# Projections of the attention as one continuous stream, one PSUM pool, and TensorE in program order

## The chip, the cores and the metric

The kernel runs on one core of a Trainium2 chip. The metric is the device time of one execution in microseconds (us). PE is TensorE (PEld its weight loads), DVE is VectorE, ACT is ScalarE, POOL is GpSimd, and SP is the engine that issues most DMAs.

## The reference

Two layers on a sequence of 1024 rows of width 1024, in float32. Layer 0 mixes with forgetting attention, layer 1 with a spatial gating MLP. A gated convolutional MLP follows each. The change touches layer 0's attention only:

```python
proj = h @ w_in                                   # 1024 x (4*1024 + 16)
q, k, v, o, fl = jnp.split(proj, [D, 2*D, 3*D, 4*D], axis=-1)
q = rmsnorm(q.reshape(B, S, 16, 64), q_gain); k = rmsnorm(k..., k_gain)
F = jnp.cumsum(log_sigmoid(fl + b_f), axis=1)
for qb in range(8):                               # blocks of 128 queries, causal
    logits = q_block @ k[:end].T * scale + F[t] - F[s], masked
    outs.append(softmax(logits) @ v[:end])
x = x + gate * ((att * sigmoid(o)) @ w_out)
```

## The kernel before

Every float32 operand of a product is split into a high and a low part (`pair`: ACT casts the high part at L126, DVE subtracts for the low part at L119), and each product is three matmuls (`mm3`, recorded at L104). A framework turns the program into one static instruction list per engine. Each engine executes its list in that order, waiting where an operand or a buffer isn't ready. Unless instructions are chained to each other, the framework's planner chooses the order of a list.

The attention runs over 8 pairs of heads, called p. For each pair the work is:

- the projection of q, k and v (`proj`): two halves of 512 rows, each of 4 blocks of 128 rows. A block is 8 steps of three matmuls with 384 columns, into a PSUM tile `pj`. A step is one `yield` of a generator. So one pair has 64 steps, or 192 matmuls. ACT copies `pj` to the tile `qkv` (L566). After a half, ACT squares it (L572), DVE sums (L574), takes a reciprocal root by a dozen small operations (L141 to L150) and multiplies (L580). The weights (8 pairs of `x` tiles) come through the buffer `fraw`;
- `heads_qk(rw, half)`: 8 transposes on PE into `ms` tiles, then ACT (L647, L653) and DVE (L649) write the operands `qq`, `kh`, `kl`. `heads_v` casts v into `w`;
- `scores(p, fb, qt)` for the 8 blocks of queries: matmuls into PSUM tiles `s`, DVE adds the bias that POOL prepared and takes the extreme (L715), ACT takes the exponential (L726), ACT or DVE divides (L730, L732);
- `values(p, g, hd)`: for each pair of key blocks up to 4 transposes into `ms`, the split into `pt` by ACT (L750) and DVE (L119), and a deferred `product` of up to 4 matmuls into the PSUM tile `pv`.

The projection of pair p+1 is the filler between the steps of pair p. `tick(w)`, called inside `scores` and `values`, draws about w steps of the generator `self.fill`. At the end of a pair `heads_qk(rw, 0)` stands ahead of `drain()` and `heads_qk(rw, 1)` follows shortly after. The generators only set the program's order; in this kernel the planner may place PE's instructions otherwise. For the last pair the filler is `out_early`, three quarters of the output projection, after `x_transposed` has brought x into the transposed layout. The rest of the output projection follows the attention.

PSUM holds three pools in the attention: 3 tiles `s`, 2 tiles `pj`, 1 tile `pv` (and 2 `ms`). Ahead of all this stand the norm, the projection of pair 0, the `o` projections and eight jobs that compute the modulation vectors (`ada_part`, L257 to L285: weights by DMA, a chain on DVE, then small matmuls at L277). The chain on `ms` tiles puts the first transposes of pair 0 behind the last of these jobs.

Of the kernel before, what the change touches and what calls it, by code (L numbers as in the profile page):

```python
# [18 lines left out]
P = 128  # L19
# [7 lines left out]
SG = 8  # L27
# [40 lines left out]
class Trunk:  # L68


    def __init__(self, ctx, tc, **io):
        self.ctx, self.tc, self.nc = ctx, tc, tc.nc
        self.__dict__.update(io)
        self.chains = {}
        self.strict = self.ordered = False
        self.pending = None
        self.hooks = []
        self.ra, self.rx = "a", "X"
        self.n = 0
# [23 lines left out]
    def mm(self, out, lhsT, rhs, start, stop):  # L103
        i = self.nc.tensor.matmul(out, lhsT, rhs, start=start, stop=stop, skip_group_check=self.strict)  # L104
        return self.chain("pe", i) if self.strict else i
# [47 lines left out]
    def transpose4(self, srcs):  # L153

        ps = self.tile(self.ms, [P, 512], F32, "ms")
        for j, s in enumerate(srcs):
            i = self.nc.tensor.transpose(ps[: s.shape[1], j * P : (j + 1) * P], s, self.ident)  # L157
            if j == 0:
                self.chain("ms", i)
        return ps  # L160
# [182 lines left out]
    def fox(self):  # L343
# [9 lines left out]
        with ExitStack() as es:  # L353
# [20 lines left out]
            def ps1(pool, tag):  # L374
                return pool.tile([P, 512], F32, tag=tag, name=self.name(tag))
# [22 lines left out]
            def raw_pieces():  # L398
# [7 lines left out]
                return [T([P, 2, 2, 256], F32, "pt", 2) for _ in range(2)]  # L406
# [65 lines left out]
            for p in range(3):  # L472
                for half in range(2):
                    acc[p, half] = ps1(*((ps_s, "s") if p == 0 else (ps_p, "pj")) if p < 2 else (ps_s, "s") if half else (ps_v, "pv"))
# [28 lines left out]
            def o_out(p, half, ps):  # L503
                t = T([P, 512], F32, "pt", 2)
# [7 lines left out]
            def o_proj(p):  # L512
                w = o_weights(3 * D + p * P)
                ps = [ps1(ps_s, "s"), ps1(ps_p, "pj")]
# [15 lines left out]
            def weights(p):  # L530
                ws = []
                n = 400 if p == 0 else 384
                for k0 in range(0, KT, 2):
                    raw = T([P, 2, 400], F32, "fraw", 2)
                    for t in range(3):
                        i = nc.sync.dma_start(
                            raw[:, :, t * P : (t + 1) * P],
                            w_in[k0 * P : (k0 + 2) * P, t * D + p * P : t * D + (p + 1) * P].rearrange(
                                "(k p) f -> p k f", p=P
                            ),  # L540
# [3 lines left out]
                    if p == 0:  # L544
                        nc.sync.dma_start(
                            raw[:, :, 384:], w_in[k0 * P : (k0 + 2) * P, 4 * D :].rearrange("(k p) f -> p k f", p=P)
                        )
                    for j in range(2):
                        t = self.xslot([P, 2, 400], F32R)
                        ws.append(self.pair(t[:, :, :n], raw[:, j, :n], "x"))  # L550
                return ws

            def proj(p, ws, rw):

                n = 400 if p == 0 else 384
                for half in range(2):
                    r = T([P, 4, 384], F32, "qkv", 3)
                    for s in range(4):
                        ps = ps1(ps_p, "pj")
                        ss = slice(s * P, (s + 1) * P)  # L560
                        for k in range(KT):
                            self.mm3(
                                ps[:, :n], [(h[half, k][0][:, ss], h[half, k][1][:, ss], *ws[k])], k == 0, k == KT - 1
                            )
                            yield
# [54 lines left out]
            self.fill, self.due = iter(()), 0.0  # L620

            def tick(w):
                self.due += w
                while self.due >= 1:
                    self.due -= 1
                    next(self.fill, None)

            def drain():
                for _ in self.fill:
                    pass  # L630
                self.due = 0.0

# [29 lines left out]
            def heads_v(rw):  # L662
                v = self.wslot([P, NST, 256])
                for half in range(2):
                    vs = rw[half][:, :, 256:384].rearrange("p s (g d) -> p s g d", d=DH)
                    vd = v[:, 4 * half : 4 * half + 4, :].rearrange("p s (g d) -> p s g d", d=DH)
                    i = nc.scalar.copy(vd[:, :, 0:4:3, :], vs)
                    if half == 0:
                        self.chain("w", i)
                    self.split_lo(vd[:, :, 1:3, :], vs, vd[:, :, 0:4:3, :])  # L670
                return v
# [12 lines left out]
            def scores(p, fb, qt):  # L684
# [22 lines left out]
                for j, (c0, c1) in enumerate(zip(cuts, cuts[1:])):  # L707
                    n = c1 - c0
                    pss = [ps1(ps_s, "s") for _ in range(2)]
# [24 lines left out]
            def values(p, g, hd, v):  # L734
# [7 lines left out]
                pv = ps1(ps_v, "pv")  # L742
                for kt in range(0, 2 * g + 2, 2):
# [5 lines left out]
                    pt = T([P, 2, 512], F32R, "pt", 2)  # L749
# [37 lines left out]
            self.fill = proj(0, weights(0), rw)  # L787
# [33 lines left out]
            def out_early():  # L821
                for ps in (range(4), range(4, PC)):
                    for n in range(2):
# [4 lines left out]
                        for half in range(2):  # L828
                            for m in range(4 * n, 4 * n + 4):
                                yield from out_mm(ps1(ps_p, "pj"), ps, m, half)  # L830

            def x_transposed():
                self.xt = {(k, half): self.xslot([P, D]) for half in range(2) for k in range(4)}
                for half in range(2):
                    xs = []
                    for st in range(4 * half, 4 * half + 4):
                        t = self.hslot(F32).rearrange("p a f -> p (a f)")
                        self.chain("h", nc.sync.dma_start(t, self.x[0, st * P : (st + 1) * P, :]))
                        xs.append(t)
                    for k in range(KT):  # L840
                        ps = self.transpose4([t[:, k * P : (k + 1) * P] for t in xs])
                        o = self.xt[k % 4, half][:, k // 4 * 512 : (k // 4 + 1) * 512]
                        i = nc.scalar.copy(o, ps)
                        if k < 4:
                            self.chain("x", i)

            fb = f_rows(0)
            heads_qk(rw, 0)
            heads_qk(rw, 1)
            v = heads_v(rw)  # L850
            for p in range(8):
                if p < 7:
                    rw = []
# [7 lines left out]
                if p == 0:  # L861
                    scores(p, fb, 0)
                else:
                    values(p - 1, 3, 1, v0)
                    v = heads_v(rw0)
                scores(p, fb, 1)
                for g in range(3):
                    scores(p, fb, 2 * g + 2)
                    values(p, g, 0, v)
                    scores(p, fb, 2 * g + 3)  # L870
                    values(p, g, 1, v)
                v0, rw0 = v, rw
                if p < 7:
                    fb = f_rows(p + 1)
                    heads_qk(rw, 0)
                    drain()
                values(p, 3, 0, v)
                if p < 7:
                    heads_qk(rw, 1)
                    scores(p + 1, fb, 0)  # L880
                else:
                    values(p, 3, 1, v)
            flush()
            drain()
            for i in range(2):
# [3 lines left out]
            for half in range(2):  # L889
                for m in range(KT):  # L890
# [7 lines left out]
                    for _ in out_mm(banks() if banks else ps1(ps_p, "pj"), range(PC, 8), m, half):  # L898
# [648 lines left out]
    def sgu(self, jobs, every, scales, nxt):  # L1547
# [6 lines left out]
        bns = self.const.tile([P, NST, SG, 6], F32, name="bns")  # L1554
# [228 lines left out]
```

## Time and profile before

| | |
|---|---|
| median of 3 runs | 2730.57 us (2730.3 to 2733.01) |
| profiled execution | 2729.37 us, its span 2727.6 us |
| mean granted PE clock | 0.972 |
| PE, PEld, DVE, ACT, POOL busy | 2582.4, 2189.0, 2092.0, 1460.2, 164.5 us |
| last o projection on PE | ends at about 171.5 us |
| first transposes of pair 0's q and k | 193.6 us |
| the same of pairs 1 to 7 | 253.8, 328.0, 407.4, 479.8, 558.7, 630.2, 697.4 us |
| last matmul of the attention's output projection | ends at about 840 us |

The times of transposes are those of the first instruction of `heads_qk(rw, 0)` on PE. From one to the next is one period of the attention. The busy time of PE is an upper bound: matmuls overlap in the records, and at half clock the same matmul counts twice as long.

### The profile page before, as it was taken

How to read it: one execution, taken by the hardware profiler on the slowest of the kernel's cores; microseconds unless marked ns; L12 is line 12 of the kernel's file. 1: busy time of each engine (PE TensorE's matmuls, PEld its weight loads, DVE VectorE, ACT ScalarE, POOL GpSimd, SP SyncE). 2: the span in 40 equal slices, each digit the busy share in tenths (PEclk: the TensorE clock that was granted, in tenths of full speed). 3: DMA queues.
4: the chain of work that ended last, by engine and by line, in shares of the span. 5: the costliest groups of instructions: out<-in, count | busy, mean ns of one | idle time of the engine just before them, and what ended most of it. 6: DMA issues, size and time to landing. Idle time of an engine off the chain costs nothing.

```text
span 2727.6 us, 35317 instructions
## 1 busy us (share of the span) xinstructions
PE 2582.4 (95%) x12522; PEld 2189.0 (80%) x12522; DVE 2092.0 (77%) x3630; ACT 1460.2 (54%) x2310; POOL 164.5 (6%) x289
## 2 busy tenths in 40 slices
PE   6999899998797899999999999999999999999997
PEld 5999888886685788888888878888877788888886
DVE  7467777678786888898688777666788888877875
ACT  7327666667654554454545654554456455545444
POOL 1012222223100000000000000000000000000000
PEclk8999999988897999999999999999999999999999
DMA  6572111131113144554846346557552343337562
GB/s 229 169 241 62 43 51 47 45 110 62 56 55 124 62 132 135 161 159 151 289 152 206 97 136 184 188 183 278 158 173 85 112 143 101 124 101 283 162 198 91
DMA packets 315512, 377.61 MB, mean 138 GB/s; under 512 B 18760, under 2 KB 196040, under 8 KB 315336
## 3 DMA queue, kind: packets, MB, share of 16 engines
q1 hardware_dynamic: 315112, 375.30, 42.1%
q8 instruction: 98, 1.61, 0.2%
q14 instruction: 78, 0.64, 0.1%
q10 hardware_dynamic: 224, 0.06, 0.0%
HBM read 285.57 MB, written 89.72 MB: 138 GB/s over the span
## 4 chain that ended last, share of the span: by engine, by line
PE 82%; DVE 10%; ACT 2%; issue 2%; DMA 2%; SPq 1%; POOL 0%; DVEq 0%; POOLq 0%; ACTq 0%
PE bankX L104 19%; PE banka L104 17%; PE bankY L104 17%; PE pj L104 14%; PE ms L104 5%; PE s L104 3%; PE ms L157 3%; PE pv L104 2%; DVE ow L994 1%; DVE hc L994 1%; DVE x L994 1%; PE ms L1600 1%; DVE x L1479 1%; DVE rw L994 1%; SPq L421 1%
## 5 line engine op out<-in xcount | busy, mean ns | idle before, releaser
L981 ACT CAST ow<-rw 128x1024 fp32r<-128x1024 f32 (+1 forms) x438 | 398.7, 911 | 474.6 <-PE bankX L104 156.3
L994 DVE TENSOR_TENSOR ow<-rw,ow 128x1024 fp32r<-128x1024 f32 (+1 forms) x438 | 457.7, 1046 | 171.9 <-ACT ow L981 171.4
L104 PE MATMUL bankX<-hc,ow 128*128 128x512 f32 x1920 | 470.3, 393 | 17.5 <-DVE ow L994 9.6
L104 PEld LDWEIGHTS bankX<-hc,ow 128*128 128x128 f32 x1920 | 361.0, 189 | 95.4 <-DVE ow L994 11.4
L104 PE MATMUL banka<-hc,ow 128*128 128x512 f32 x1608 | 393.4, 393 | 6.5 <-ACT hc L981 2.8
L104 PE MATMUL bankY<-hc,ow 128*128 128x512 f32 x1584 | 388.6, 392 | 0.8 <-DVE ow L994 0.8
L104 PEld LDWEIGHTS banka<-hc,ow 128*128 128x128 f32 x1608 | 301.1, 189 | 71.3 <-ACT hc L981 4.4
L104 PEld LDWEIGHTS bankY<-hc,ow 128*128 128x128 f32 x1584 | 296.5, 188 | 64.3 <-issue 1.9
L104 PE MATMUL pj<-x,h 128*128 128x384 f32 (+1 forms) x1536 | 302.0, 346 | 6.5 <-ACT qkv L566 6.5
L104 PEld LDWEIGHTS pj<-x,h 128*128 128x128 f32 x1536 | 272.8, 192 | 9.7 <-ACT qkv L566 7.5
L1479 DVE SCALAR_TENSOR_TENSOR x<-x,prm,x 128x1023 f32<-128x1023 f32 (+1 forms) x160 | 204.3, 1279 | 2.7 <-ACT x L1477 2.1
L104 PE MATMUL bankY<-ow 128*128 128x512 f32 x720 | 203.6, 391 | 0.2 <-DVE x L998 0.2
L104 PE MATMUL banka<-ow 128*128 128x512 f32 x672 | 187.3, 391 | 0.5 <-DVE x L998 0.5
L104 PEld LDWEIGHTS bankY<-ow 128*128 128x128 f32 x720 | 135.2, 188 | 28.5 <-DVE x L998 0.6
L104 PE MATMUL bankX<-ow 128*128 128x512 f32 x588 | 156.3, 392 | 0.0
L104 PEld LDWEIGHTS banka<-ow 128*128 128x128 f32 x672 | 125.8, 188 | 27.3 <-ACT x L1028 0.8
L104 PE MATMUL pv<-pt,w 128*128 128x256 f32 (+1 forms) x640 | 124.4, 309 | 18.6 <-DVE pt L119 10.1
L104 PE MATMUL ms<-ow 128*128 128x512 f32 x546 | 139.9, 390 | 0.9 <-DVE pp L994 0.9
L119 DVE TENSOR_TENSOR pt<-ms,pt 128x512 fp32r<-128x512 f32 (+1 forms) x160 | 100.1, 631 | 47.7 <-ACT pt L750 46.6
L104 PEld LDWEIGHTS pv<-pt,w 128*128 128x128 f32 x640 | 103.2, 208 | 33.5 <-DVE pt L119 16.4
L104 PEld LDWEIGHTS bankX<-ow 128*128 128x128 f32 x588 | 110.8, 188 | 23.9 <-issue 1.0
L104 PEld LDWEIGHTS ms<-ow 128*128 128x128 f32 x546 | 102.0, 188 | 23.7 <-DVE pp L994 2.9
(299 smaller groups left out, 3883.5 us busy)
## 6 DMA issues: line engine op xcount, KB each, us to landing
rw<-yd SPq DMA_DIRECT2D x210, 256.0 KB
rw<-in_ffn_w_up_dram SPq DMA_DIRECT2D x88, 512.0 KB
yd<-pp SPq DMA_DIRECT2D x60, 512.0 KB
rw<-in_ada_w_dram SPq DMA_DIRECT2D x48, 512.0 KB
rw<-in_ffn_w_down_dram SPq DMA_DIRECT2D x88, 256.0 KB
rw<-in_sgu_w_in_dram SPq DMA_DIRECT2D x32, 512.0 KB
yd<-x SPq DMA_DIRECT2D x30, 512.0 KB
fraw<-in_fox_w_in_dram SPq DMA_DIRECT2D x96, 128.0 KB
```

The costliest lines, as they stand in the source:

```text
L104: i = self.nc.tensor.matmul(out, lhsT, rhs, start=start, stop=stop, skip_group_check=self.strict)
L119: return (eng or self.nc.vector).tensor_tensor(lo, full, hi.bitcast(F32), op=ALU.subtract)
L157: i = self.nc.tensor.transpose(ps[: s.shape[1], j * P : (j + 1) * P], s, self.ident)
L421: i = nc.sync.dma_start(r[:, :, t, :], src[:, :, t, q * 256 : (q + 1) * 256])
L981: return self.ao(self.nc.scalar.copy(t[:, 0], src))
L994: return self.vo(self.nc.vector.tensor_tensor(out, a, b, op=op))
L1479: stt(o[:, j:], a[:, : S - j], w[2 - j], o[:, j:], op0=ALU.mult, op1=ALU.add)
L1600: k = nc.tensor.matmul(px[:, b * P : (b + 1) * P], vn[:, b, c * P : (c + 1) * P], sg[:, 0], start=True, stop=True)
```

## The change

1. The three PSUM pools become one of 6 tiles (`fps`), from which `s`, `pj`, `pv`, the o projections' `o` and the output projection's `op` are all taken.
2. From the first `heads_qk` to the end of the attention every matmul and transpose is chained to the one before (`inorder`): PE executes in the order in which the program is written.
3. The projections of pairs 1 to 7, then `x_transposed`, then `out_early` are one generator, `stream`. `tick` draws 0.85 steps per unit (1.4 after the last projection). It is not drained per pair; `until(p, half)` draws the steps that a half still lacks, twice per pair.
4. The second half of a pair's projection is consumed inside that pair's own period: `heads_qk(rws[p], 1)` stands after `scores(p, fb, 3)`, and `heads_v` is done by halves.
5. The weights of the next pair are loaded and split during the last block of the current projection, two `x` tiles after each second step.
6. `pt` has 3 buffers for 2, and a product is issued when more than two are pending, not one. `bns`, a small tile of layer 1, moves to another SBUF pool.

```diff
+        return self.chain("pe", i) if self.strict or self.inorder else i
...
-            ps_s = es_p.enter_context(tc.tile_pool(name="fs", bufs=3, space=PSUM, reuse_waits="tile"))
-            ps_p = es_p.enter_context(tc.tile_pool(name="fpj", bufs=2, space=PSUM, reuse_waits="tile"))
-            ps_v = es_p.enter_context(tc.tile_pool(name="fpv", bufs=1, space=PSUM, reuse_waits="tile"))
+            ps_f = es_p.enter_context(tc.tile_pool(name="fps", bufs=6, space=PSUM, reuse_waits="tile"))
...
+                load(0)
+                load(1)
+                yield
+                for j in range(4):
+                    for i in range(2):
+                        t = self.xslot([P, 2, 400], F32R)
+                        ws.append(self.pair(t[:, :, :n], raws[j][:, i, :n], "x"))
+                    if j < 2:
+                        load(j + 2)
+                    yield
...
+            def proj(p, ws, rw, nw=None):
...
+                        if nw and half == 1 and s == 3:
+                            next(nw)
                         for k in range(KT):
+                            yield
                             self.mm3(...)
+                            if nw and half == 1 and s == 3 and k % 2:
+                                next(nw)
...
-            self.fill, self.due = iter(()), 0.0
+            self.fill, self.due, self.rate = iter(()), 0.0, 0.85
             def tick(w):
-                self.due += w
+                self.due += w * self.rate
...
+            def until(p, half):
+                while len(rws[p]) <= half:
+                    next(self.fill)
...
+            def stream():
+                ws = []
+                nw = weights(1, ws)
+                for _ in nw:
+                    pass
+                for p in range(1, 8):
+                    ws2 = []
+                    nw = weights(p + 1, ws2) if p < 7 else None
+                    yield from proj(p, ws, rws[p], nw)
+                    ws = ws2
+                self.rate = 1.4
+                yield from x_transposed()
+                yield from out_early()
...
                     tick(1)
-                    if len(later) > 1:
+                    if len(later) > 2:
                         later.pop(0)()
-                        tick(1)
+                    tick(1)
...
-            heads_qk(rw, 0)
-            heads_qk(rw, 1)
-            v = heads_v(rw)
+            self.inorder = True
+            self.fill = stream()
+            heads_qk(rws[0], 0)
+            scores(0, fb, 0)
             for p in range(8):
-                if p < 7:
-                    rw = []
-                    self.fill = proj(p + 1, weights(p + 1), rw)
-                else:
-                    x_transposed()
-                    for i in range(2):
-                        out_w(range(4), i)
-                        out_y(range(4), i)
-                    self.fill = out_early()
...
+                if p:
+                    values(p - 1, 3, 1, v0)
+                v = self.wslot([P, NST, 256])
+                heads_v(rws[p], v, 0)
+                scores(p, fb, 1)
+                until(p, 1)
+                scores(p, fb, 2)
+                values(p, 0, 0, v)
+                scores(p, fb, 3)
+                heads_qk(rws[p], 1)
+                values(p, 0, 1, v)
+                heads_v(rws[p], v, 1)
+                scores(p, fb, 4)
...
+                scores(p, fb, 6)
+                if p < 7:
+                    until(p + 1, 0)
+                values(p, 2, 0, v)
+                scores(p, fb, 7)
+                values(p, 2, 1, v)
                 if p < 7:
                     fb = f_rows(p + 1)
-                    heads_qk(rw, 0)
-                    drain()
+                    heads_qk(rws[p + 1], 0)
                 values(p, 3, 0, v)
                 if p < 7:
-                    heads_qk(rw, 1)
                     scores(p + 1, fb, 0)
```

Three places show what moves. In the rows `MATMUL a<-b,c` writes a, and a transpose is a MATMUL with `ident`. The number after a name tells tiles of one name apart.

The first place is PE between the o projections and the first scores. Before, the planner put the projection of pair 1 (`pj`) ahead of and between the first transposes of `qkv`:

```order
L104 MATMUL pj_2147<-x_1682,h_413 128x384 x3
L104 MATMUL pj_2147<-x_1685,h_433 128x384 x3
L104 MATMUL pj_2147<-x_1692,h_484 128x384 x3
L104 MATMUL pj_2147<-x_1695,h_522 128x384 x2
L277 MATMUL ms_1557<-ones,tm_1534 128x1 x4
L157 MATMUL ms_1633<-ident,qkv_806 128x128 x4
L104 MATMUL pj_2147<-x_1695,h_522 128x384
L104 MATMUL pj_2147<-x_1702,h_574 128x384 x3
```

Now, on the same engine at the same place:

```order
L104 MATMUL o_1568<-h_646,x_1564 128x512 x3
L279 MATMUL ms_1432<-ones,tm_1391 128x1 x4
L279 MATMUL ms_1522<-ones,tm_1415 128x1 x4
L279 MATMUL ms_1545<-ones,tm_1504 128x1 x4
L279 MATMUL ms_1551<-ones,tm_1528 128x1 x4
L157 MATMUL ms_1627<-ident,qkv_800 128x128 x4
L157 MATMUL ms_1636<-ident,qkv_800 128x128 x4
L104 MATMUL s_1659<-kh_738,qq_737 128x128
```

No projection is left between the last o projection and the first scores. Before, 107 matmuls of pair 1's projection stood ahead of the first transposes, and 150 of its 192 ahead of the first scores.

The second place is PE at the end of a period, where the next pair's first half is transposed (`qkv`, here from pair 0 to 1 before). Before, no filler step is left between the last products and the transposes:

```order
L157 MATMUL ms_2342<-ident,raw_1909 128x128
L157 MATMUL ms_2342<-ident,raw_2006 128x128 x2
L104 MATMUL pj_3086<-x_2585,h_652 128x384 x2
L104 MATMUL pv_2312<-pt_2318,w_1673 128x256 x4
L104 MATMUL pj_3086<-x_2585,h_652 128x384
L104 MATMUL pv_2312<-pt_2329,w_1673 128x256 x4
L157 MATMUL ms_2363<-ident,qkv_1738 128x128 x4
L104 MATMUL pv_2312<-pt_2346,w_1673 128x256
L157 MATMUL ms_2372<-ident,qkv_1738 128x128 x4
```

Now (here between pairs 2 and 3) filler steps go on through the place:

```order
L157 MATMUL ms_4117<-ident,cv_3697 128x128
L157 MATMUL ms_4117<-ident,cv_3787 128x128 x2
L104 MATMUL pj_4113<-x_3370,h_427 128x384 x3
L104 MATMUL pv_4089<-pt_4095,w_3504 128x256 x4
L104 MATMUL pj_4113<-x_3420,h_478 128x384 x3
L157 MATMUL ms_4138<-ident,qkv_3495 128x128 x4
L157 MATMUL ms_4147<-ident,qkv_3495 128x128 x4
L104 MATMUL pv_4089<-pt_4106,w_3504 128x256 x4
```

The third place is new: the second half of pair 2 is transposed inside its own period. On PE:

```order
L104 MATMUL pj_3632<-x_3370,h_423 128x384 x3
L104 MATMUL pv_3594<-pt_3599,w_3504 128x256 x2
L104 MATMUL pv_3594<-pt_3599,w_3504 128x128 x2
L157 MATMUL ms_3655<-ident,qkv_3053 128x128 x4
L157 MATMUL ms_3664<-ident,qkv_3053 128x128 x4
L157 MATMUL ms_3676<-ident,cv_3350 128x128
L157 MATMUL ms_3676<-ident,raw_3513 128x128 x2
L104 MATMUL pj_3632<-x_3420,h_474 128x384 x3
L104 MATMUL pj_3632<-x_3423,h_512 128x384 x3
L104 MATMUL s_3703<-kh_738,qq_737 128x512
```

And on DVE, what these transposes wait for (the multiply of `qkv_3053`) and what follows them:

```order
L148 TENSOR_TENSOR rs_t_3481<-rs_y_3480 128x16
L760 RECIPROCAL lr_3652<-ll_3650 128x1
L149 TENSOR_TENSOR rs_t_3481<-rs_t_3481,rs_vh_3479 128x16
L764 TENSOR_SCALAR cv_3611<-cv_3611,lr_3652 128x512
L150 SCALAR_TENSOR_TENSOR rs_y_3480<-rs_t_3481,rs_y_3480 128x16
L593 TENSOR_TENSOR qkv_3053<-qkv_3053,rs_y_3480 128x4x256
L799 TENSOR_TENSOR av_3593<-pv_3594,av_3593 64x256
L684 SCALAR_TENSOR_TENSOR qq_737<-ms_3655,qg_134_731,qq_737 64x512
```

Before, both halves were transposed near the period's end, and the planner had put the second half behind the values of the last query blocks. Now the chain copy, square, sum, root, multiply of a second half stands between its last `pj` and these transposes, with 10 filler steps and three blocks of scores in between on PE.

More of the change, by code (lines that the diff above doesn't have):

```diff
@@ L660, in flush, with heads_v @@
                     later.pop(0)()
[L662 to L671, printed above, removed]
+            def heads_v(rw, v, half):
+                vs = rw[half][:, :, 256:384].rearrange("p s (g d) -> p s g d", d=DH)
+                vd = v[:, 4 * half : 4 * half + 4, :].rearrange("p s (g d) -> p s g d", d=DH)
+                i = nc.scalar.copy(vd[:, :, 0:4:3, :], vs)
+                if half == 0:
+                    self.chain("w", i)
+                self.split_lo(vd[:, :, 1:3, :], vs, vd[:, :, 0:4:3, :])
             def f_rows(p):
@@ L708, in scores @@
                     n = c1 - c0
[L709 removed]
+                    pss = [ps1("s") for _ in range(2)]
                     for hd in range(2):
```

95 lines of the change are left out of this document (46 added, 49 removed).

## The prediction

> **What bounds the kernel now.** I read the page first, for the 40 slices of the span.
>
> ```profile
> PE   6999899998797899999999999999999999999997
> ...
> PEclk8999999988897999999999999999999999999999
> ```
>
> TensorE is at nine tenths nearly everywhere, so it bounds the kernel. The attention (slices 4 to 12) has sevens and eights, and the granted clock falls there too. Second, I cut the attention into stretches at the transposes of each pair's first half. The columns are stretch, length, then busy time of PE, PEld, DVE, ACT, POOL with instruction counts, granted clock, DMA share, GB/s.
>
> ```profile
> 171.50:193.60 22.10, 22.10 (x141) 22.10 (x139) 15.90 (x27) 3.67 (x8) 9.74 (x14) 1.00 0.68 244
> 193.60:253.80 60.20, 60.20 (x382) 58.75 (x382) 47.37 (x145) 44.25 (x89) 14.22 (x24) 1.00 0.17 53
> 253.80:328.00 74.20, 65.04 (x411) 61.28 (x410) 53.46 (x155) 47.73 (x98) 16.22 (x29) 0.98 0.15 43
> 328.00:407.40 79.40, 70.15 (x410) 65.58 (x409) 56.95 (x166) 50.47 (x103) 20.40 (x38) 0.89 0.18 54
> 407.40:479.80 72.40, 66.36 (x410) 62.37 (x409) 53.18 (x153) 47.57 (x98) 16.85 (x28) 0.96 0.17 50
> 479.80:558.70 78.90, 70.20 (x410) 65.58 (x409) 58.05 (x169) 50.45 (x102) 20.57 (x36) 0.88 0.16 49
> 558.70:630.20 71.50, 65.95 (x411) 62.02 (x410) 52.23 (x154) 47.55 (x98) 16.35 (x26) 0.97 0.29 100
> 630.20:697.40 67.20, 55.85 (x290) 46.89 (x289) 55.83 (x164) 49.05 (x98) 20.65 (x39) 0.85 0.21 71
> 697.40:740.00 42.60, 31.88 (x183) 26.16 (x184) 23.88 (x54) 28.32 (x58) 1.54 (x4) 0.92 0.13 42
> 740.00:840.00 100.00, 100.00 (x525) 84.65 (x523) 77.24 (x162) 44.96 (x84) 12.92 (x22) 1.00 0.21 74
> ```
>
> The reader is to see three things. Six periods take 443.6 us, 73.9 each. In the five full ones PE stands idle for 5.5 to 9.3 us, and those at clock 0.88 or 0.89 keep PE busy 4 to 5 us longer for the same 410 instructions. The period from 630.2 has 120 instructions fewer on PE and is still 67.2 us, with DVE at 83%: without filler the softmax chain sets the pace. Third, the waits of PE over these six periods (waiter, releaser, total us, times, longest):
>
> ```profile
> PE s L104 <- DVE smx L715: 15.5, 11, 2.8
> PE pv L104 <- DVE pt L119: 9.9, 17, 1.5
> PE ms L157 <- DVE pt L119: 6.6, 10, 1.8
> PE pj L104 <- ACT qkv L566: 6.5, 6, 1.7
> PE pv L104 <- DVE av L767: 5.0, 8, 1.0
> ```
>
> Last, where a period spends its time: PE is full while filler lasts, and hungry after it.
>
> ```profile
> 300.00:310.00 10.00, 10.00 (x70) 9.66 (x69) 8.09 (x28) 5.55 (x12) 2.40 (x4) 1.00 0.04 13
> 310.00:340.00 30.00, 20.61 (x104) 17.64 (x104) 24.27 (x74) 20.26 (x36) 6.99 (x12) 0.83 0.16 58
> 415.00:460.00 45.00, 45.00 (x294) 44.29 (x294) 28.72 (x82) 27.91 (x64) 11.20 (x20) 1.00 0.16 45
> ```
>
> So there is a surplus of filler first and none later, and the change spreads it.
>
> **PE's work at full clock.** Prices come from runs of one kind (start, length, instruction, count):
>
> ```profile
> 185.75 7.20 PE L104 MATMUL pj<-x,h 128*128 128x384 f32 x40
> 722.13 1.04 PE L157 MATMUL ms<-ident,h 128*128 128x128 f32 x8
> 804.45 1.20 PE L104 MATMUL pv<-pt,w 128*128 128x256 f32 x8
> 809.60 22.20 PE pj L104 x96
> ```
>
> Less the overlapping tail of the last one, that is 0.176 us for a projection matmul (0.53 a step), 0.11 for a transpose, 0.13 for a product, and 0.231 for 512 columns. A period has 192 projection matmuls (33.8), 88 transposes (9.7), 80 products (10.4) and 36 x 512 columns of scores (8.3): 62.2 us for 408 instructions, 0.152 each. The stretch 415 to 460 gives 0.153.
>
> **The change part by part.**
>
> *The start.* The first transposes wait for the last modulation job, and the first scores come 9 us later:
>
> ```profile
> 193.60 0.63 PE L157 MATMUL ms<-ident,qkv 128*128 128x128 f32 x4
> 202.44 0.22 PE L104 MATMUL s<-kh,qq 128*128 128x128 f32 x1
> ```
>
> PE filled all of it with pair 1's projection. In the new order nothing can stand there, so 22.1 us from 171.5 and the chain to the first scores are idle. The two sets of transposes now follow each other (before, 18 projection matmuls lay between), so I set the first scores at 199. The lost work, 150 matmuls or 26 us, is done later, inside the periods below.
>
> *Period 0.* Up to pair 1's transposes there are 60 units of `tick`, hence 51 steps (27), scores 8.3, 48 products (6.2), 58 transposes (6.4): 48 us, plus 5 of waits like those below. It ends at 252, level with 253.8 before, but with 153 projection matmuls done since 171.5. Before, the groups of the two stretches ahead of it show 336:
>
> ```profile
> L104 PE MATMUL pj<-x,h 128*128 128x384 f32 x107 | 19.6, 339 | 0.0
> L104 PE MATMUL pj<-x,h 128*128 128x384 f32 x229 | 45.7, 341 | 0.0
> ```
>
> The 183 that are missing cost 32 us. That is the debt that the six periods and the end must earn back before anything is gained.
>
> *Periods 1 to 6.* 76 units x 0.85 are 64.6 steps for 64 needed, so filler neither runs out nor piles up. PE's 62.2 us are the floor. To it I add the waits that the written order forces:
> First, the second half's transposes come 10 steps (5.3), 9 x 512 columns (2.1), 12 products and 3 transposes (1.9) after the last `pj`: 9.3 us. They need a chain on ACT and DVE:
>
> ```profile
> L566 ACT COPY qkv<-pj 128x384 f32<-128x384 f32 x44 | 20.5, 477 | 25.8 <-PE pj L104 25.6
> L572 ACT ACTIVATE cv<-qkv 128x1024 f32<-128x1024 f32 x6 | 6.4, 1059 | 0.0
> L574 DVE TENSOR_REDUCE qk_ss<-cv 128x16 f32<-128x1024 f32 x6 | 7.3, 1209 | 0.0
> L148 DVE TENSOR_TENSOR rs_t<-rs_y 128x16 f32<-128x16 f32 x35 | 7.6, 218 | 0.1
> L580 DVE TENSOR_TENSOR qkv<-qkv,rs_y 128x1024 f32<-128x1024 f32 x12 | 15.6, 1301 | 0.1
> ```
>
> Alone it takes 0.5 + 1.1 + 1.2 + 13 x 0.2 + 1.3 = 6.7 us, no wait at all. But 42 DVE instructions stand from the first scores of this stretch to the multiply. At a period's average (53.46 / 155 = 0.345) they need 14.5, a wait of 5.2 us or a little more. About half are one to 16 columns wide, so I take 12, nearer the upper end. With 0.3 until the first of those scores is written, less the cover of 9.3, PE waits 3.0 us.
> Second, `scores(p, 4)` follows after 2 steps and needs DVE's third operand write:
>
> ```profile
> L649 DVE SCALAR_TENSOR_TENSOR qq<-ms,qg,qq 64x512 fp32r<-64x512 f32 x24 | 18.0, 749 | 4.6 <-ACT qq L647 4.1
> L647 ACT ACTIVATE qq<-ms,qg 64x512 fp32r<-64x512 f32 x24 | 16.4, 681 | 8.6 <-PE ms L157 8.3
> ```
>
> 0.7 + 3 x 0.75 after transposes against 1.4 of cover: 1.5. The first half's operands release the `ms` tiles equally late behind the exponentials of 1024 columns: another 1.5 (0 to 3).
> Third, the old waits: 15.5 + 6.5 were for PSUM tiles, which six shared ones cover unless DVE falls behind; 9.9 for `pt` go with the deferral by one more product; the others shown, 6.6 + 5.0, stay: 1.9 a period. I add 0.4 for the clock, since even the best of the full periods was at 0.96 to 0.98.
> Together 70.5 us. The ends are 65, where the first three waits are nearly hidden, and 75, where the first is 5.2 and everything behind it is late. For while PE stands at the third place, filler that is ready stands behind the transposes and can't pass, and DVE and ACT get no new scores; before, the planner had put filler there.
> *Loads and the rest.* The weights move to the last block of a pair's projection:
>
> ```profile
> 420.26 7.80 SPq L536 DMA_DIRECT2D fraw<-in_fox_w_in_dram  x12
> 423.48 0.93 ACT L126 CAST x<-fraw 128x384 fp32r<-128x384 f32 x2 [0.48 <-DMA fraw<-in_fox_w_in_dram]
> ```
>
> 3.2 us from issue to use. Two of four loads are issued a period ahead, the other two some 4 us ahead of their casts: nothing, at worst 1 us a period. SP holds only `so` and `nat` behind them, which nobody needs within 5 us. POOL works 16 to 21 us a period and stays free; half-by-half `heads_v` and `bns` move work of the same size and cost nothing.
>
> *The end.* After pair 7's transposes PE still has 9 steps (4.8), 64 transposes of x (7.0), 384 output matmuls (88.7; before 24 of them had been done), scores 8.3, 112 products 14.6, 118 transposes 13.0: 136.4. Before, 10.7 us were idle here (697.4 to 740). Now ACT's 16 copies of x and the first output operands follow the last projection just as closely, in pair 7's third place. I take the 10.7 again, the 4.5 of that place and 1 of small ones: 16 us of waits (10 if x comes early, since its loads are issued ahead; 22 if the copies delay ACT's exponentials), so 152.
>
> Sum: 252 + 6 x 70.5 + 152 = 827 against 840: 13 us off the profiled 2729.4 (span 2727.6 and 1.8 around it). The median of the runs is 1.2 us above that execution, so **2718 us**.
>
> **The rivals.** *The spread hides the chain entirely:* a period of 65. For it: PE full for 45 us with DVE at 64%. Against: DVE needs 52 to 58 of the 65. It gives 794 at the end, 2685.
> *DVE's queue sets the third place:* if the 42 instructions run at the average, the wait is 5.2, and a clock drop after it 1.7: with the delay handed on to DVE's next block the period is 75: the end at 854, 2745. It decides from 72.7, which is (840 - 252 - 152) / 6. For it: DVE at 83% already paces the period of 67.2.
> *The clock:* it drops after hungry slices.
>
> ```profile
> 255.00:260.00 5.00, 2.60 (x16) 2.46 (x17) 3.75 (x7) 3.55 (x8) 0.00 (x0) 1.00 0.00 0
> 315.00:320.00 5.00, 1.61 (x12) 1.22 (x12) 5.00 (x19) 4.21 (x7) 1.43 (x2) 1.00 0.17 61
> 320.00:325.00 5.00, 4.51 (x22) 4.03 (x22) 4.72 (x26) 2.62 (x5) 0.00 (x0) 0.66 0.20 73
> ```
>
> An idle 2.4 us leaves it at 1.00, 3.4 us in five brings 0.66. If my 3.0 us at the third place does it each time, half a clock over some 3.4 us costs 1.7 a period, 10 in all: 2728, no change.
> The Trainium skill ("TensorE: Matmul & The Clock Gate", section "HAM oscillation — how this bites in real kernels") says to leave no gap above about 3.4 us, since the window runs freely. By it the clock holds at a gap of 3.0 and falls with one of 5; these slices agree.
>
> **Chances.** Main case 45%, hidden chain 20%, DVE's queue 20%, clock 15%. The range takes the hidden chain and the queue at their values: 2684 to 2745; the main case alone spans 2702 to 2733 (periods of 68 to 73). Below 0.2% (5.5 us) this kernel's runs can't tell a change from none. Faster: 36 + 20 + 4 = 60%; same 7 + 1 + 7 = 15%; slower 2 + 19 + 4 = 25%.
>
> **What would show it.** Right: an idle PE from 171 to about 194; pair 1's transposes near 252, then every 70 to 71 us; PE busy 62 to 65 of it, clock near 1.00; waits of `ms` on the multiply and `s` on DVE's operands; hardly any for PSUM. Wrong: periods above 73, a clock of 0.9, or new waits of `s` or `pj` on their readers.

## The result and the profile after

The changed kernel takes 2774.43 us (median of 4 runs, 2772.33 to 2775.91) against 2730.44 for the kernel before on the same chip: a ratio of 1.016 with a 95% interval of 1.0147 to 1.0172. It is 44 us slower, where 13 us faster was forecast. The profiled execution has a span of 2771.5 us at a mean granted clock of 0.968. The output projection's last matmul ends at about 882.5 us instead of 840. The stage behind it starts as it did: its first matmuls wait 9.70 us in both traces. So 42 of the 44 us are lost by then, in the attention and its output projection. In the page's 40 slices of the span (busy share of PE in tenths, and the granted clock in tenths) slices 4 to 10 are now all eights, where five of these seven were nines before:

```profile
PE   6978888888797899999999999999999899999998
...
PEclk9989999999998899999999999999999999999999
```

Then the stretches of the changed kernel, in the columns of the prediction's table (length, busy PE, PEld, DVE, ACT, POOL, clock, DMA share, GB/s), cut again at the transposes of each pair's first half: the start, the period of pair 2, that of pair 4, the six periods together, and the end.

```profile
171.50:189.10 17.60, 5.33 (x24) 5.25 (x25) 14.18 (x24) 0.00 (x0) 9.07 (x14) 0.52 0.75 269
...
328.20:412.90 84.70, 69.04 (x412) 65.84 (x411) 59.65 (x167) 49.71 (x102) 19.63 (x35) 0.90 0.17 51
491.00:568.90 77.90, 67.03 (x412) 63.63 (x410) 57.96 (x167) 49.62 (x101) 20.53 (x36) 0.93 0.18 55
...
249.90:721.60 471.70, 401.95 (x2463) 382.04 (x2462) 339.94 (x961) 293.89 (x600) 111.46 (x192) 0.93 0.18 56
721.60:882.50 160.90, 144.62 (x768) 121.75 (x766) 108.76 (x230) 78.67 (x151) 15.61 (x28) 0.96 0.21 70
```

PE is busy for only 5.3 of the start's 17.6 us, and period 0 ends at 249.9, both about as forecast. The six periods take 471.7 us, 78.6 each where 70.5 was forecast. PE is idle for 69.75 of them (471.70 - 401.95), 11.6 a period, and busy 67.0 a period where full clock needs 62.2. The waits of PE in these six periods (waiter, releaser, total us, times, longest) give nearly the whole idle time a name:

```profile
PE ms L157 <- DVE qq L684: 34.6, 12, 3.9
PE ms L157 <- DVE qkv L593: 12.1, 6, 4.0
PE ms L157 <- DVE pt L119: 10.4, 9, 2.9
PE ms L157 <- ACT cv L762: 5.3, 2, 2.9
PE ms L157 <- ACT raw L762: 4.3, 2, 2.3
PE pv L104 <- DVE pt L119: 2.4, 2, 1.3
PE ms L157 <- DVE kl L684: 0.4, 2, 0.2
```

Half of it is one wait, met twice a period: a transpose of `values` needs an `ms` tile that DVE has not finished reading for `qq`. At the third place of the change (pair 4's second half) the timeline shows PE, ACT and DVE so (start, length, engine, instruction, count, idle time before it and its releaser):

```profile
506.07 1.30 PE L104 MATMUL pj<-x,h 128*128 128x384 f32 x6
...
524.64 1.09 PE L157 MATMUL ms<-ident,qkv 128*128 128x128 f32 x8 [1.72 <-DVE qkv L593]
528.88 0.45 PE L157 MATMUL ms<-ident,raw 128*128 128x128 f32 x1 [3.15 <-DVE qq L684]
529.41 2.27 PE L104 MATMUL pj<-x,h 128*128 128x384 f32 x6
```

```profile
525.34 0.68 ACT L682 ACTIVATE qq<-ms,qg 64x512 fp32r<-64x512 f32 x1 [0.72 <-PE ms L157]
525.92 0.67 ACT L682 ACTIVATE kh<-ms,prm 64x512 fp32r<-64x512 f32 x1
526.62 0.62 ACT L688 CAST kh<-kh 64x512 fp32r<-64x512 f32 x1
527.26 0.68 ACT L682 ACTIVATE qq<-ms,qg 64x512 fp32r<-64x512 f32 x1
...
526.05 0.74 DVE L684 SCALAR_TENSOR_TENSOR qq<-ms,qg,qq 64x512 fp32r<-64x512 f32 x1 [0.59 <-ACT qq L682]
526.83 0.74 DVE L684 SCALAR_TENSOR_TENSOR kl<-ms,prm,kh 64x512 fp32r<-64x512 f32 x1
527.98 0.76 DVE L684 SCALAR_TENSOR_TENSOR qq<-ms,qg,qq 64x512 fp32r<-64x512 f32 x1 [0.41 <-ACT qq L682]
```

The eight transposes fill both `ms` tiles. The first tile comes free when DVE's second write of `qq` has read it, and that follows the fourth ACT instruction: 0.68 + 0.67 + 0.62 + 0.68, then 0.76 on DVE. Directly behind the eight, in program order, stands a transpose that wants that tile. Projection steps stand behind it, and the chained PE may not take them first. The clock falls with the gap (slices of 3 us, same columns as the stretches):

```profile
524.00:527.00 3.00, 1.09 (x8) 0.85 (x8) 2.38 (x6) 2.22 (x5) 0.00 (x0) 1.00 0.00 0
527.00:530.00 3.00, 1.12 (x5) 1.15 (x6) 2.08 (x3) 2.32 (x5) 0.56 (x1) 0.56 0.00 0
530.00:533.00 3.00, 3.00 (x10) 2.71 (x9) 0.99 (x2) 0.27 (x1) 1.62 (x4) 0.50 0.00 0
533.00:536.00 3.00, 3.00 (x18) 2.90 (x18) 0.97 (x4) 0.58 (x2) 0.00 (x0) 0.81 0.00 0
```

So the six projection matmuls at 529.41 take 2.27 us, and the six at 506.07 took 1.30. The same happens at a period's end, with one gap alone: behind the transposes of pair 4's first half, at 490.99, PE works until 492.90, is idle for 3.07 us, and the slice behind the gap is at 0.50.

```profile
495.97 0.63 PE L157 MATMUL ms<-ident,cv 128*128 128x128 f32 x4 [3.07 <-DVE qq L684]
...
497.00:500.00 3.00, 3.00 (x12) 2.90 (x11) 1.38 (x3) 1.33 (x3) 0.00 (x0) 0.50 0.14 44
```

### The profile page after: what moved, and what is told of

The parts are those of the page before. It is cut to its first block, busy times and chain, and to the rows that moved or that the text cites. A ratio compares the mean times of both kernels' runs of the same rounds, so it can differ in the third digit from the quotient of the medians.

```text
span 2771.5 us, 35276 instructions
## 1 busy us (share of the span) xinstructions
PE 2579.8 (93%) x12522; PEld 2193.2 (79%) x12522; DVE 2103.1 (76%) x3630; ACT 1458.0 (53%) x2310; POOL 164.8 (6%) x289
## 4 chain that ended last, share of the span: by engine, by line
PE 78%; DVE 13%; ACT 4%; DMA 3%; issue 2%; SPq 0%; POOL 0%; DVEq 0%; ACTq 0%; POOLq 0%
PE bankX L104 19%; PE banka L104 17%; PE bankY L104 17%; PE pj L104 7%; PE ms L104 5%; PE ms L157 3%; PE op L104 3%; PE s L104 2%; PE o L104 2%; PE pv L104 2%; DVE ow L1037 1%; DVE hc L1037 1%; DVE x L1037 1%; PE ms L1643 1%; DVE tm L270 1%
## 5 line engine op out<-in xcount | busy, mean ns | idle before, releaser
L104 PE MATMUL pj<-x,h 128*128 128x384 f32 (+1 forms) x1536 | 339.9, 359 | 0.0
L157 PE MATMUL ms<-ident,cv 128*128 128x128 f32 x364 | 78.2, 297 | 49.0 <-DVE qq L684 27.6
L782 ACT CAST pt<-ms 128x512 fp32r<-128x512 f32 (+1 forms) x160 | 85.4, 540 | 49.7 <-PE ms L157 47.0
```

What stands on the lines that cost most here:

```text
L782: nc.scalar.copy(pt[:, 0, :nb], ps[:, :nb])
```

## The experiments

The theory "order" says: a chained PE may not step over a transpose that waits, no filler stands behind `heads_qk`, and the clock falls after each gap. The rival "DVE's queue" says: the softmax chain on DVE and ACT is late anyway, and a gap that is filled at one place opens at another. The kernel before, timed beside each run, took 2729.4 to 2731.2 us, so a difference between two runs is good to about 2 us.

**The clock alone.** Matmuls whose result nobody reads stand behind the transposes of every `heads_qk`.

```diff
+                warm = ps1("s")
+                for i in range(18):
+                    self.mm(warm[:, :384], h[0, 0][0][:, :P], h[0, 1][0][:, :384], True, True)
                 flush()
```

> The changed kernel with 18 matmuls whose result nobody reads (384 columns, 3.2 us) behind the transposes of each heads_qk, where PE stands waiting. No useful work is moved. Theory (clock): the busy time of PE, 67 us a period against 62.2 of work at full clock, is matmuls at half clock after these gaps. Then the clock rises from 0.93 to 0.97 or more, a period falls by some 3.5 us although the extra work is as long as the gap, and the time is about 2753 (2745 to 2763). Rival (the gap alone costs): nothing is gained and the extra matmuls lengthen what they don't cover: 2774 to 2785.

Measured 2753.98 us, ratio to before 1.0086 (1.0069 to 1.0103): 20 us less than the changed kernel for more work. The six periods run at clock 0.99, and the waits on `qq` shrink from 34.6 to 0.3 us.

```profile
248.41:702.09 453.68, 419.91 (x2678) 401.54 (x2677) 339.48 (x961) 294.39 (x600) 109.27 (x192) 0.99 0.18 56
...
PE ms L157 <- DVE qq L684: 0.3, 1, 0.3
```

DVE and ACT did the changed kernel's work in 18 us less (453.7 against 471.7). The extra matmuls are 12 x 18 in these periods, 38 us at 0.176 each. Without them PE is busy for 382 us instead of 402, and they and the idle time left make 72 us, as long as the changed kernel's idle 70. So about 20 us of the loss is work done at a lower clock.

**Useful work in the gap.** The same place gets six projection steps, drawn from the stream, and `tick` draws fewer.

```diff
-            self.fill, self.due, self.rate = iter(()), 0.0, 0.85
+            self.fill, self.due, self.rate = iter(()), 0.0, 0.69
...
+                for _ in range(6):
+                    next(self.fill, None)
                 flush()
```

> The changed kernel with 6 filler steps written right behind the 8 transposes of each heads_qk, and 0.69 steps per unit of tick instead of 0.85, so that a period still draws about 64. Theory (order): PE loses its time at the two heads_qk of a period, because the next transposes stand right behind them and need an ms tile that DVE's write of qq has not yet released; the clock falls in that gap. Then these waits (34.6 us in six periods) fall under 8 us, the clock goes to about 0.98, a period goes from 78.6 to about 71 and the time to about 2730 (2720 to 2742). Rival (DVE's queue): DVE paces the period, and PE will wait as long at other places: periods of 76 or more, a time of 2760 or more.

Measured 2721.98 us, ratio 0.9971 (0.9958 to 0.9984), 52 us less than the changed kernel. Periods are 73.2 us, where about 71 was expected; they give 33 us, and the rest comes from period 0 and the end, which have the same place. The waits on `qq` fall from 34.6 to 9.2 us (under 8 was expected), but those on the split of the softmax weights, `pt`, rise from 12.8 in all to 42.1. This list is from 245 to 700 us, 17 us beyond the six periods; within them `pt` has 40.8:

```profile
PE ms L157 <- DVE pt L119: 33.1, 22, 3.6
PE ms L157 <- DVE qq L684: 9.2, 6, 2.2
PE pv L104 <- DVE pt L119: 9.0, 10, 2.1
```

The place is the one that "order" names. The rival holds in part: waits open in `values`, seemingly because filler that is spent at `heads_qk` is missing there.

**The start.** 31 steps of pair 1's projection stand ahead of the first transposes, and `tick` draws at 0.82.

```diff
+            for _ in range(32):
+                next(self.fill)
             heads_qk(rws[0], 0)
```

> The changed kernel with 31 steps of pair 1's projection written ahead of the first transposes, and 0.82 steps per unit so that the lead is given back slowly. Theory (order): the idle start is a debt of its own: 16 us of PE work move into the idle time from 171 to 189, and as the periods don't change (78 us), the end comes 16 us earlier: about 2758. Rival (DVE's queue): the number of steps left does not set the time of a period, so nothing is gained until the last projection, and at most 5 us at the end: 2770.

Measured 2756.33 us, ratio 1.009 (1.0075 to 1.0105): 18 us less than the changed kernel. PE is full to the first transposes, and the waits on `qq` stay (36.9 us in 11). The time is as expected, the way to it is not: pair 1's transposes come later (256.1 for 249.9), the periods shrink a little (76.5 us for 78.6), and the stretch behind them is 9 us shorter.

```profile
171.50:190.60 19.10, 19.10 (x123) 19.10 (x123) 14.92 (x25) 2.15 (x5) 8.45 (x12) 1.00 0.73 264
```

**Both.** 26 draws at the start, six steps of cover, rate 0.66.

> Both edits of the cover and the start together (25 steps ahead of the first transposes, 6 more behind them and behind every later heads_qk, 0.66 steps per unit). Theory (order): both gains add, 2774 less 44 less 16, about 2714 (2700 to 2728), which would beat both kernels. Rival (DVE's queue): 2755 or more.

Measured 2718.87 us, ratio 0.9953 (0.9938 to 0.9968). The two gains, 52 and 18, don't add: beside the cover the start is worth 3 us. Waits on `pt` are 35.0 us in its six periods (22.3 + 12.7), not much less than the 40.8 with cover alone. That speaks for the rival within this order.

**PE freed.** The changed kernel with the planner's order on PE.

```diff
-            self.inorder = True
+            self.inorder = False
```

> The changed kernel without the chaining of PE's instructions: the planner chooses PE's order again, everything else is as changed (one pool, the stream, the second half inside its own period, pt with 3 buffers). Theory (order): the written order is what costs; the planner puts filler into the gaps and the idle start, and the time is 2700 to 2735. Rival (structure): the later second half and the stream themselves cost, whoever orders PE: 2755 or more.

Measured 2735.37 us, ratio 1.0016 (1.0006 to 1.0025), at the upper end of what "order" gave. Chaining costs 39 us here, and everything else in the change 5. But the planner didn't find all: the start stays idle, and the tiles held by `qq` still stop it.

```profile
171.50:190.40 18.90, 5.26 (x28) 5.09 (x28) 14.91 (x25) 0.70 (x2) 9.11 (x14) 0.62 0.76 275
...
PE ms L157 <- DVE qq L684: 20.1, 10, 3.2
PE pv L104 <- ACT pt L782: 14.5, 12, 2.3
```

**Chaining alone.** The kernel before with PE chained in its own program order.

```diff
-        return self.chain("pe", i) if self.strict else i
+        return self.chain("pe", i) if self.strict or self.inorder else i
...
+            self.inorder = True
```

> The kernel before with nothing but the chaining: PE keeps the order in which the old program is written, old pools, old filler. Theory (order): a written order without filler behind the transposes costs, whichever program it comes from; here all filler of a pair is drawn at one step per unit and both heads_qk of a period stand with little behind them: 2750 to 2780. Rival (the new place of the second half is what costs): the old order is harmless, 2725 to 2740.

Measured 2832.58 us, ratio 1.0372 (1.0357 to 1.0388): 102 us slower, far more than expected. The first halves' transposes of pairs 1 to 7 go from 256.6 to 775.2, so a period has 86.4 us instead of 73.9, and the six make 75 of the 102. The two largest of its waits from 250 to 820 us:

```profile
PE pv L104 <- DVE pt L119: 26.7, 40, 1.5
PE ms L157 <- DVE qkv L582: 21.9, 7, 4.4
```

The values' split is waited for 40 times; it seems that a deferral by one product is too short in the written order. The second half's transposes wait for the multiply, 2.5 to 4.4 us each time, which the planner had given cover. The wait for `ms` tiles held by `qq` is there too, with 16.6 us in 12. The new program order is thus a better one to chain (39 us lost) than the old (102).

**PSUM tiles of their own.** In the changed kernel the transposes of `heads_qk` go into tiles `hq` of the six-tile pool.

```diff
-                    ps = self.transpose4([... for s in range(4)])
+                    ps = self.transpose4([... for s in range(4)], ps1("hq"))
```

> The changed kernel with the 16 x 8 transposes of heads_qk in tiles of the pool of six instead of the two ms tiles; order and filler as changed. Theory (order): PE waits there because the next transposes need an ms tile that DVE's qq still reads. With tiles of their own these go on at the end of a period (gain of about 3 us and of the clock behind it), while at the third place the scores still need qq: a period of about 74.5, a time of about 2750 (2740 to 2760). Rival (DVE's queue paces): the wait moves to the next tile, 2768 or more.

Measured 2732.67 us, ratio 1.0011 (1.0001 to 1.002): 42 us less than the changed kernel, with no instruction added or left out, and more than "order" had expected (2740 to 2760). The edit also leaves both `ms` tiles to `values`. The transpose of `values` no longer asks for a tile that `qq` holds; the waits on `qq` that are left are those of the scores, which need it as an operand:

```profile
251.28:688.23 436.95, 390.01 (x2463) 369.51 (x2462) 338.12 (x961) 292.16 (x600) 110.16 (x192) 0.97 0.20 61
...
PE hq L157 <- DVE qkv L593: 10.7, 5, 4.0
PE s L104 <- DVE qq L684: 10.6, 6, 2.6
```

Against the changed kernel's six periods PE is idle 46.9 instead of 69.8 us and busy 12 us less at a clock of 0.97.

**Start, cover and own tiles together.**

> Start, cover and own PSUM tiles together. In the version with start and cover, 13 us of waits on qq and kl and 22 us of waits of transposes on the split of pt were left in six periods. Theory (order): the first go and part of the second, 2 to 3 us a period: about 2704 (2695 to 2714). Rival (DVE's queue): DVE is busy for 53 to 61 of 66 to 77 us a period and PE's waits only move: 2714 to 2722.

Measured 2701.86 us, ratio 0.9895 (0.9881 to 0.991). Of the waits on `qq` 3.5 us are left, on `pt` 32.7.

```profile
PE ms L157 <- DVE pt L119: 22.9, 17, 3.9
PE pv L104 <- DVE pt L119: 9.8, 11, 2.0
PE s L104 <- DVE qq L684: 3.5, 4, 2.0
```

**The pool alone.** The kernel before with one pool of six.

```diff
-            ps_s = es_p.enter_context(tc.tile_pool(name="fs", bufs=3, space=PSUM, reuse_waits="tile"))
-            ps_p = es_p.enter_context(tc.tile_pool(name="fpj", bufs=2, space=PSUM, reuse_waits="tile"))
-            ps_v = es_p.enter_context(tc.tile_pool(name="fpv", bufs=1, space=PSUM, reuse_waits="tile"))
+            ps_s = ps_p = ps_v = es_p.enter_context(tc.tile_pool(name="fps", bufs=6, space=PSUM, reuse_waits="tile"))
```

> The kernel before with one edit of the change alone: one pool of six PSUM tiles in place of the three pools of three, two and one; old program order, TensorE ordered by the planner. Theory 'order' (the loss is made by chaining TensorE in the order of the new stream): the pools alone move little, since the six tiles are the same six banks; what they can take away are the waits of before that hang on the single tile of the weighted sums (pv behind the multiply av, 5.0 us in all) and some of the waits on smx (15.5), if these came from tiles and not from operands. Expected 2715 to 2735. Rival 'the shared pool': tiles are handed out in turn, so a tile held long (a projection's accumulation of 16 matmuls) stops the next ones in turn whatever they are for, and the pool is itself a part of the loss: 2740 to 2760.

Measured 2753.26 us, ratio 1.0087 (1.0072 to 1.0102): the pool is a loss of 24 us by itself. The rival's range came true and its reason did not: the waits on tiles of the pools are gone, as "order" had it, but `ms`, which is not in the pool, waits on `qq` for 51.6 us in 13. The kernel before (first fence) had 22 projection matmuls left behind the transposes of pair 2; with the pool of six (second) the planner has put 23 of them ahead, from 316.81 to 321.06, and none is left for the gap:

```profile
330.44 0.65 PE L157 MATMUL ms<-ident,qkv 128*128 128x128 f32 x4 [1.76 <-DVE pt L119]
330.85 0.54 PE L104 MATMUL pv<-pt,w 128*128 128x256 f32 x3
332.78 6.64 PE L104 MATMUL pj<-x,h 128*128 128x384 f32 x22 [1.39 <-ACT qkv L566]
```

```profile
316.81 4.25 PE L104 MATMUL pj<-x,h 128*128 128x384 f32 x23
...
326.88 0.66 PE L157 MATMUL ms<-ident,qkv 128*128 128x128 f32 x4 [2.60 <-DVE pt L119]
327.29 0.53 PE L104 MATMUL pv<-pt,w 128*128 128x256 f32 x3
331.23 1.09 PE L157 MATMUL ms<-ident,cv 128*128 128x128 f32 x4 [3.40 <-DVE qq L647]
```

So it seems that having only two `pj` tiles had kept filler for the place that needs it. That is read from the two traces; other sizes of the pools were not tried.

**The pool and own tiles.**

> The kernel before with one pool of six PSUM tiles (2753.3 by itself) and, beside it, the transposes of heads_qk in tiles of that pool instead of the two ms tiles. The pool alone made 13 waits of ms transposes on DVE's write of qq, 51.6 us in all, where the kernel before had hardly any. Theory 'two ms tiles': these waits are the pool's whole loss, and they go when no later transpose needs a tile that qq still holds: 2700 to 2720. Rival 'no filler left': with more tiles the planner runs the projection earlier, so that nothing but the values of the last blocks is left at that place, and PE then waits elsewhere (scores for qq, values for pt): 2740 to 2755.

Measured 2741.98 us, ratio 1.0039 (1.0024 to 1.0054). The rival was right: the waits on `qq` go, and others take their place (`pv` on DVE's `pt` 22.4 us in 22, from 247 to 701). Own tiles give 11 of the 24 us; the rest, it seems, is missing filler.

**The change with own tiles, unchained.**

> The changed kernel without chaining (2735.4 by itself) and with the transposes of heads_qk in tiles of the six-tile pool; without the 26 projection steps at the start and the 6 steps of cover, so it differs from the fastest version so far (2672.0) by these two alone. Its waits on qq through ms tiles were 20.1 us, which should go: 2710 to 2718 by these alone. Theory 'order': the planner finds the ready projection steps itself, so start and cover are worth little more than the start's idle 16 us, and this comes near 2690 to 2705. Rival: cover and start matter without chaining as they did with it (31 us beside own tiles): 2700 to 2718.

Measured 2718.54 us, ratio 0.9951 (0.9934 to 0.9968). "Order" was too hopeful, and the rival right with its upper end: the planner by itself doesn't give what start and cover give.

**Start, cover and own tiles, unchained.**

> The version with 26 projection steps ahead of pair 1's first transposes, 6 steps behind the transposes of heads_qk, and PSUM tiles of their own for these transposes (2701.9), with the chaining of TensorE taken away, so that the planner sets its order again. Theory 'order': chaining costs only where a matmul that waits stands ahead of ready ones; in the chained version the waits that are left are those on the split of the weights (pt), about 35 us in its attention stage, behind which the planner could put projections: 2680 to 2700. Rival 'DVE's queue': the weights come late because VectorE is late, so the order of TensorE doesn't matter any more: 2698 to 2706. Should the planner undo the cover by moving the filler away from heads_qk, the time rises: above 2706.

Measured 2671.98 us, ratio 0.9785 (0.9769 to 0.9802): 57 us faster than before and 102 faster than the changed kernel, below what either theory expected. The six periods take 64.8 us each (388.91 / 6), and PE is idle for 16 us of them:

```profile
247.06:635.97 388.91, 372.88 (x2403) 357.49 (x2402) 322.64 (x940) 287.91 (x593) 105.83 (x192) 0.98 0.21 65
...
PE pv L104 <- ACT pt L784: 6.2, 6, 2.4
PE ms L157 <- DVE pt L119: 4.0, 3, 2.7
...
PE pv L104 <- DVE pt L119: 0.8, 1, 0.8
```

DVE is at 83% there, and yet PE waits 4.8 us for `pt` behind DVE (and 6.2 behind ACT), against 32.7 in the chained version with the same filler. So "DVE's queue" was not a limit of DVE's speed; it showed only because a chained PE could not step past a late split. Beside own tiles, start and cover are worth 47 us without chaining (2718.5 to 2672.0) and 31 with it.

## Why the prediction was wrong, step by step

- **The start and period 0** came out right: PE nearly idle to 189.1 (194 forecast), end of period 0 at 249.9 (252). In part two errors cancel: the first scores ran at 193.2, not at 199, and from there period 0 took 56.7 us, not 53, with a wait of 3.51 us for an `ms` tile held by `qq` at 209.28.
- **The step that failed is the second added wait**, "0.7 + 3 x 0.75 after transposes against 1.4 of cover: 1.5", and its copy at the period's end, "another 1.5". The sum of both was 3.0 a period; 34.6 / 6 = 5.8 were measured, 3.2 at the third place and 2.6 at the period's end. The chain's length was about right: 2.95 forecast, 3.4 from ACT's start at 525.34 to DVE's end at 528.74. What was wrong at the third place is the cover: the two steps stand behind the `ms` transposes of `values`, and those wait for the same tile. The prediction priced the waiter as `scores(p, 4)`, which needs the operand; what waits first is a transpose, which needs only the tile. At the period's end it did name the tiles, and only the size was off (1.5 for 2.6, within its 0 to 3). The rows on PE that the third place shows had it: `ms_3676` directly behind `ms_3664`. Own tiles, which remove just this, give 42 us.
- **The clock term**, 0.4 a period, was mis-sized: PE's busy time is 67.0 against 62.2, 4.8 a period. The matmuls that nobody reads take 20 us of it away, 3.3 a period over six; what makes the other 1.5 no run shows. The rival "the clock" had set 1.7 for one gap a period; the waits on `qq` alone make two. The prediction took from the page "TensorE: Matmul & The Clock Gate" of the Trainium skill (section "HAM oscillation — how this bites in real kernels") that the clock holds at a gap of 3.0 us, since the section asks for no gap above about 3.4. Here a gap of 3.07 us alone has the clock at 0.50 behind it, and one of 3.15 us, with one of 1.72 shortly before it, at 0.56 and 0.50, so this trace does not bear out that reading.
- **The third place's wait for the multiply** was right in kind and a little large: 3.0 forecast, 12.1 / 6 = 2.0 measured. So the rival "DVE's queue", priced at 5.2 there, named a time nearer to the result (2745) for a reason that didn't occur; that it came near is luck.
- **The old waits**: those on `smx` and on `qkv` by ACT are gone, as forecast; so are those on `av`, which were forecast to stay. 1.9 a period were kept for `pt` and `av`; `pt` alone has 2.1, and ACT's divisions (L762), which had no term, 1.6.
- **The period**: idle 11.6 where the terms had 7.9, busy 67.0 where they had 62.6: together the 8.1 by which 78.6 exceeds 70.5. Six times that is 48.7 us.
- **The end** took 160.9 against 152. PE's idle time there is 16.3 (16 forecast); its busy time 144.6 (136.4 forecast), at a clock of 0.96.
- Together: -2.1 + 48.7 + 8.9 = 55.5, which is 882.5 - 827.
- **PSUM tiles**: "which six shared ones cover" was right about the waits and missed that the pool changes when filler is spent. By itself it loses 24 us, in the old program and with the planner's order; what it costs in the changed kernel no run shows.
- **The rival "the spread hides the chain entirely"** (a period of 65) was thought bounded by DVE at 52 to 58 of 65. The last experiment has 64.8 with DVE at 322.64 / 6 = 53.8: the period was there to be had, with filler behind the transposes, tiles that are not shared, and PE free to step over a late split.

## What to carry to other kernels

When an engine is put into program order, look at each instruction that stands directly behind a hand-over to other engines, and ask for its buffer as well as its operands: a buffer still being read stops everything behind it, ready or not. Give such a hand-over buffers of its own, keep filler for the instant behind it, and price the clock that falls after a gap together with the gap. Filler has to be kept, too: here a larger pool let the planner spend it early, and fewer buffers seem to have held it back.

## What the runs showed of the hardware

The granted clock fell to 0.56 in the slice (527 to 530) in which an idle time of 3.15 us ended, 1.72 us of idleness having come shortly before, and it was still at 0.50 in a slice that PE filled (530 to 533). A gap of 3.07 us with PE at work on both sides had 0.50 in the slice behind it (497 to 500), which PE filled too. Eighteen matmuls behind each `heads_qk` held the clock at 0.99 over six periods (0.93 without) and made the kernel 20 us faster for work that nobody reads.
